# A decoder layer on one core: where the masks, the first splits, the sums and the turns of x stand in the first FFN

## The chip, the core and the metric

The kernel runs on one core of a Trainium2 chip. A core has five engines, each with its own in-order queue: TensorE (PE, matrix products; PEld is its weight load), VectorE (DVE), ScalarE (ACT), GpSimd (POOL) and SyncE (SP, which here issues DMAs). Engines wait for each other through semaphores. The metric is the device time of one execution in microseconds (us); the median of several runs counts.

## The reference

One layer of a decoder trunk in float32: 16 meta tokens and 1024 real ones, width 1024, FFN width 2816. Cut to what matters:

```python
h = h + 0.5 * swiglu(rms_norm(h, ffn1_norm[l]), ffn1_w_in[l], ffn1_w_out[l])
u = rms_norm(h, mix_norm[l]) @ w_in[l]
o_hg = hgrn2(...)              # gated linear recurrence, 4 heads, lower bound lb from two rows of logits
o_sb = stick_breaking(...)     # causal attention, 8 heads
h = h + concat[o_hg, o_sb] @ w_out[l]
h = h + 0.5 * swiglu(rms_norm(h, ffn2_norm[l]), ffn2_w_in[l], ffn2_w_out[l])

def swiglu(h, w_in, w_out):
    g, u = jnp.split(h @ w_in, 2, axis=-1)
    return (jax.nn.silu(g) * u) @ w_out
```

## The kernel before, in words

**Products.** Every float32 operand is split in two: a rounded high part (an ACT copy into the type fp32r) and the rest (a DVE subtraction). A product of two operands takes three matmuls: high by high, low by high, high by low. The FFNs use a fast 2 x 2 block scheme with seven products instead of eight: the activations give the operands B11, B21, B22 and the sums T1 to T4, the weights four blocks and the sums S1 to S4. Weight sums are made by POOL from loaded blocks (`made`, L380, in `fast_in`), split by ACT (L356) and DVE (L358), and used by 12 matmuls of 128x128 by 128x512 (`times`, L426).

**The first FFN's input pass** (`fast_in`, called in `run`). Hidden columns are taken in pairs of *quads*: for each of the gate and the up half a quad makes seven products into the PSUM banks qa, qb, qc. The first four pairs, eight quads q0 to q7, are *opened*: their B11 and B21 products are made while the operands are still being prepared (`open_tokens`). Their later five products follow in `in_turns`, which takes one step of each of the two quads of a pair in each round: first the weight S2, then T2, T3, T1, T4, B22. After each opened pair `between()` is called twice. Seven further pairs run quad by quad, with `between()` after each quad.

**Orders.** TensorE's order in this stage is the one in which the program is written (`manual_schedule`). In `open_tokens` the same holds for ACT, DVE and SP. There a list of items, number 2 to 15, runs between the opened products: item i first prepares a weight for item i+2, then does `items[i]`, then the product of item i. Items 8 to 11 (`combine`) make T3's plain tiles `t3` (L797, L798), items 12 to 15 (`second`) make T2 and split it (`halve`, L306 on ACT, L307 on DVE). After the last item a loop splits the other operands in the order T3, T1, T4, B22; for T4 it first subtracts in place, `sub(b21[j], b21[j], t2[j])` (L853). Elsewhere in the stage the tile framework orders the queues of ACT, DVE, POOL and SP itself, by readiness and by place in the program. `issue_after(x)` puts an instruction behind x on x's engine.

**What starts when the opening is over** (`open_ev` in `run`). `setup_rest` loads the small vectors, makes `ident_b`, `neg_b` and the seven masks of the recurrence (for each level a DVE memset of `sd`, four POOL selects, L119 and L123, and a DVE cast to `masks`, L127), and the few operations on the lower bound's logits. Then the pool of the opening's plain tiles (b11, b21, b22, t2, t3) is closed and new pools take its space: the evictions, `turn_x` (row and result of a transposed piece of x) and `early` (blocks loaded early; the second quad of an opened pair takes its raw blocks and sums from it). A tile in a reused place waits until the old tile's last reader is done.

**Two side jobs run inside the pass.** `turn_x` turns x by TensorE in 18 pieces, one in each `between()`: the first call loads a row (`xrow`, one buffer), each later call transposes it (L918), copies it out (L922), stores it (L923) and loads the next. `split_ahead` splits weights of later stages ahead of time and stores both parts in DRAM; for the second FFN's first columns `quad_group` makes the sums S1 to S4 on POOL (L197), with their split on ACT (L172) and DVE (L173).

**The output pass** (`fast_out`) follows with eleven steps q for each of seven block products, beginning with step "A12". Each q loads a weight block (`raw`) and an activation (`act`), splits both (`halved`, L605 on ACT and L606 on DVE) and makes 12 matmuls (L660). `self.apart` is true in the first FFN and false in the second. The norm before the mixer ends with casts in `norm_steps` (L1755), after which `self.lb` and `self.lbc`, two sigmoids of `self.mx` (L1936, L1937), are written in the program; the recurrence's gates use them later.

Of the kernel before, what the change touches and what calls it, by code (L numbers as in the profile page):

```python
# [15 lines left out]
AF = mybir.ActivationFunctionType  # L16
# [24 lines left out]
class Block:  # L41
# [59 lines left out]
    def setup_rest(self):  # L101

        nc = self.nc
        for dst, src in self.loads:
            nc.sync.dma_start(dst, src)
        nc.vector.tensor_copy(self.ident_b, self.ident)
        nc.vector.memset(self.neg_b, 0.0)
        nc.gpsimd.affine_select(
            out=self.neg_b, in_=self.neg_b, pattern=[[-1, P]],
            compare_op=ALU.is_gt, fill=NEG, base=0, channel_multiplier=1,  # L110
        )
        sd = self.sd
        for i, n in enumerate(LEVELS):
            nc.vector.memset(sd, 1.0)
            nb = P // (2 * n)
            for h in range(2):
                v = sd.rearrange("s (b h r) -> s b h r", h=2, r=n)[:, :, h, :]
                at = n * (1 - h)
                nc.gpsimd.affine_select(  # L119
                    out=v, in_=v, pattern=[[-2 * n, nb], [0, n]],  # L120
                    compare_op=ALU.is_ge, fill=0.0, base=-at, channel_multiplier=1,
                )
                nc.gpsimd.affine_select(  # L123
                    out=v, in_=v, pattern=[[2 * n, nb], [0, n]],
                    compare_op=ALU.is_gt, fill=0.0, base=at + n, channel_multiplier=-1,
                )
            nc.vector.tensor_copy(self.masks[:, i, :], sd)  # L127

        nc.vector.tensor_scalar_mul(self.qg8, self.qg, 1.0 / 8.0)
        l0, l1, mx = self.l0, self.l1, self.mx  # L130
        nc.vector.tensor_max(mx, l0, l1)
        nc.vector.tensor_sub(l0, l0, mx)
        nc.vector.tensor_sub(l1, l1, mx)
        nc.vector.tensor_sub(mx, l0, l1)

    def weights(self, name, raw, split, ctx, on_vector=False):
        self.wp = self.pool(name, ctx=ctx)
# [48 lines left out]
    def quad_group(self, pool, w_in, col, dst):  # L186

        nc = self.nc
        views = [
            w_in[512 * h : 512 * h + 512, col + P * i : col + P * i + P]  # L190
            .rearrange("(k p) f -> p k f", p=P) for i, h in ((0, 0), (1, 0), (1, 1), (0, 1))
        ]
        s = {}

        def kept(name, op, x, y):
            t = s[name] = pool.tile([P, 512], F32, tag="sum", name="sum", bufs=2)
            op(t, x, y)  # L197
            return t

        add, sub = nc.gpsimd.tensor_add, nc.gpsimd.tensor_sub  # L200
        return views, [
            (dst[0], lambda r: r[0]),
            (dst[1], lambda r: r[3]),
            (dst[4], lambda r: kept(1, add, r[1], r[2])),
            (dst[2], lambda r: kept(2, sub, s[1], r[0])),
            (dst[6], lambda r: kept(4, sub, r[3], s[2])),
            (dst[5], lambda r: r[2]),
            (dst[3], lambda r: kept(3, sub, r[0], r[1])),
        ]
# [136 lines left out]
    def fast_in(self, ops, n, w_in, actD, openers, ev0, open_ev, feed=None, meta=None, spare=None,  # L346
                between=lambda: None, after_opened=lambda: None, taken=lambda at, step=True: None):

        nc = self.nc
# [194 lines left out]
            ]  # L544

        def in_turns(live):
            while live:
                live = [q for q in live if next(q, live) is not live]

        opened = [q for f in range(0, 2 * openers, 2) for q in pair(f, "first")]  # L550
        if feed:
# [10 lines left out]
        ev["p"] = open_ev()  # L562
        for i in range(0, 2 * openers, 2):
            in_turns(opened[i : i + 2])
            between()
            between()
        after_opened()
        for f in range(2 * openers, D_FF // P, 2):
# [4 lines left out]
    def fast_out(self, hT, cs, n, w_out, actD, ready, between=lambda a, q: None,  # L573
                 meta=lambda a, q, blocks: None):

        nc = self.nc
# [24 lines left out]
        def halved(src, name, m):  # L601
            i = turns[name]
            turns[name] = (i + 2) % 8
            hi, lo = (self.parts[name][:, j, :m] for j in (i, i + 1))
            nc.scalar.copy(hi, src)  # L605
            nc.vector.tensor_sub(lo, src, hi.bitcast(F32))  # L606
            return hi, lo

        sub = nc.vector.tensor_sub
# [36 lines left out]
        for bank, a, b, start, (i, j) in steps:  # L646
            if start:
                banks[bank] = [
                    pout.tile([P, n], F32, tag=f"{bank}{m}", name="o") for m in range(4)
                ]  # L650
            for q in range(nq):
                src, blocks = left(a, q)
                wh, wl = halved(src, "w", 512)
                xh, xl = halved(right((q, b), n), "t", n)
                order = [(m, e) for m in range(4) for e in range(3)]
                if a == "A12" and q == 0:
                    order.sort(key=lambda me: me[1])
                for m, e in order:
                    y, z = ((wh, xh), (wl, xh), (wh, xl))[e]
                    nc.tensor.matmul(  # L660
                        banks[bank][m], y[:, m * P : (m + 1) * P], z,
                        start=start and q == 0 and e == 0,
                        stop=q == nq - 1 and e == 2, skip_group_check=True,
                    )
# [52 lines left out]
    def open_tokens(self, ops, opened, rows_at, pool, operands):  # L717
# [92 lines left out]
        def second(j):  # L810
            if j == 0:
                rows_at.close()
                operands()
            sub(t2[j], b22[j], b11[j])
            self.halve(ops["T2"], t2[j], j)

        def roots():
            for i, row in enumerate(rb + [meta]):
# [9 lines left out]
        def sums(i):  # L828
# [6 lines left out]
            5: roots,  # L835
            6: lambda: (spare(4, 5), scales()),
            7: keep_b22,
            12: lambda: second(0), 13: lambda: second(1),
            14: lambda: second(2), 15: lambda: second(3),
        }  # L840
        items.update({8 + j: lambda j=j: combine(j) for j in range(4)})
        after = {6: turn_b22, 7: turn_b12, 8: turn_meta}
        for i in range(2, len(order)):
            if i + 2 < len(order):
                next(order[i + 2])
            items[i]()
            next(order[i])
            after.get(i, lambda: None)()
        left = iter((("T3", t3), ("T1", b11), ("T4", b21), ("B22", b22)))
        for o, b in left:  # L850
            for j in range(4):
                if o == "T4":
# [715 lines left out]
    def run(self):  # L1568
# [12 lines left out]
        n = 512  # L1581
# [8 lines left out]
        with ExitStack() as c0:  # L1590
            with ExitStack() as c1:
# [122 lines left out]
                with tc.manual_schedule(engines={nc.tensor.engine}), ExitStack() as c2:  # L1714
# [17 lines left out]
                    def norm_steps(t0, banks, engines, wait, turn):  # L1732

                        acc = pn.tile([P, n], F32, tag="nacc", name="nacc", bufs=2)
                        for k in range(KT):
                            self.square(acc, hT, k, t0, n, pn, engines[k % 2])
                            nc.gpsimd.dma_start(hD[k, :, t0 : t0 + n], hT[:, k, t0 : t0 + n])
                            yield
                        for _ in range(wait):
                            yield  # L1740
                        r = self.inv_rms_rows(acc, n, pn, *banks()[0])
                        for _ in range(turn):
                            yield
                        ps = self.spread_rows(r, n, pn, *banks()[1])
                        rs = pn.tile([P, n], F32, tag="spread", name="rs", bufs=2)
                        nc.scalar.copy(rs, ps)
                        yield
                        for k in range(KT):
                            t = pn.tile([P, n], F32, tag="nt", name="nt", bufs=2)
                            nc.vector.scalar_tensor_tensor(  # L1750
                                t, hT[:, k, t0 : t0 + n], self.gm[:, k : k + 1], rs,
                                ALU.mult, ALU.mult,
                            )
                            xh, xl = hat
                            nc.scalar.copy(xh[:, k, t0 : t0 + n], t)  # L1755
# [180 lines left out]
                nc.scalar.activation(self.lb, self.mx, AF.Sigmoid)  # L1936
                nc.scalar.activation(self.lbc, self.mx, AF.Sigmoid, scale=-1.0)  # L1937

                def after_early():
                    pe_ctx.close()  # L1940
# [233 lines left out]
```

## Time and profile before

| | us |
|---|---|
| median of 3 runs (2066.33 to 2069.84) | 2068.24 |
| profiled execution | 2067.01 |
| its span, from first to last instruction | 2065.3 |
| first FFN, input pass: first product to first product of the output pass | 15.9 to 532.7 |
| TensorE busy in the span | 1982.5 |

The profile gives start and length of each instruction on each engine, and for idle time what ended it (the releaser). "Granted clock" is the share of TensorE's full clock that it was given. A row of a stretch gives its length and then the busy time of PE, PEld, DVE, ACT and POOL, with instruction counts in brackets, then the granted clock, the share of the DMA engines and GB/s. A row of waits reads: who waited, for whom, total us, times, longest. A row of the order of time reads: start, length, engine, line, operation, what it writes and reads, count, and in square brackets the idle time ahead of it with its releaser.

### The profile page before, as it was taken

To read this page: it belongs to the slowest core of one execution; us is meant where nothing else is said; L and a number is where in the kernel's file an instruction comes from. 1 tells how busy PE (TensorE), PEld (TensorE's weight loads), DVE (VectorE), ACT (ScalarE), POOL (GpSimd) and SP (SyncE) were. 2 spreads that over 40 slices of the span, in tenths; PEclk is the share of its full clock that TensorE was granted. 3 is DMA by queue.
4 is the path that set the end of the run, shared out by engine and by line. 5 is a ranking of instruction groups with operands and counts; after the bars stand their busy time and mean duration, and the time that the engine had idled before them with its cause. 6 is when DMAs were issued, how large, how long until landed. Compare 5 with 4: busy or idle time off the path is not lost.

```text
span 2065.3 us, 30888 instructions
## 1 busy us (share of the span) xinstructions
PE 1982.5 (96%) x11004; PEld 1659.6 (80%) x11004; DVE 1361.4 (66%) x1988; ACT 867.7 (42%) x1758; POOL 672.8 (33%) x768
## 2 busy tenths in 40 slices
PE   7598999999999999999999998999999999999998
PEld 6387788777788888888889887878888888888887
DVE  6675467887677764235767668548576776676774
ACT  6332334333344443446666654535033233234443
POOL 0466345665200001224333323321264464440000
PEclk9799999999999999999999999999999999999999
DMA  6144487764896522634454337684633332359463
GB/s 185 56 129 147 148 263 247 260 227 164 276 328 228 166 94 87 206 125 137 121 140 132 100 109 246 167 242 156 203 118 95 112 105 94 107 217 321 131 199 137
DMA packets 283097, 347.18 MB, mean 168 GB/s; under 512 B 28016, under 2 KB 183152, under 8 KB 282944
## 3 DMA queue, kind: packets, MB, share of 16 engines
q1 hardware_dynamic: 263376, 287.98, 44.1%
q0 software_dynamic: 18528, 57.23, 7.9%
q8 instruction: 87, 1.43, 0.3%
q14 instruction: 66, 0.54, 0.1%
q10 hardware_dynamic: 1040, 0.00, 0.0%
HBM read 233.75 MB, written 111.38 MB: 167 GB/s over the span
## 4 chain that ended last, share of the span: by engine, by line
PE 68%; DVE 4%; DMA 2%; ACT 1%; issue 1%; SPq 0%; DVEq 0%
PE o L660 18%; PE qb L426 9%; PE qc L426 6%; PE qa L426 6%; PE proj L247 5%; PE proj L249 5%; PE proj L248 5%; PE flip L1300 2%; PE wo L248 1%; PE wo L247 1%; PE wo L249 1%; DMA raw<-in_ffn_w_out_dram 1%; PE lvl L1096 1%; PE oacc L1370 1%; PE oacc L1372 1%
## 5 line engine op out<-in xcount | busy, mean ns | idle before, releaser
L426 PE MATMUL qb<-T,wh 128*128 128x512 f32 x1056 | 350.4, 396 | 31.5 <-ACT wh L356 24.7
L426 PEld LDWEIGHTS qb<-T,wh 128*128 128x128 f32 x1056 | 201.7, 191 | 80.2 <-ACT wh L356 27.2
L358 DVE TENSOR_TENSOR wl<-s,wh 128x512 fp32r<-128x512 f32 x160 | 209.5, 1310 | 80.9 <-ACT wh L356 79.4
L426 PE MATMUL qa<-B,wh 128*128 128x512 f32 x696 | 229.7, 394 | 0.6 <-ACT B L755 0.2
L660 PE MATMUL o<-t,w 128*128 128x512 f32 x924 | 215.9, 394 | 2.8 <-DVE t L606 1.8
L247 PE MATMUL proj<-xh,wh 128*128 128x512 f32 (+2 forms) x640 | 216.6, 338 | 0.8 <-DVE st L996 0.7
L249 PE MATMUL proj<-xl,wh 128*128 128x512 f32 (+2 forms) x640 | 209.7, 328 | 0.8 <-DVE xl L1756 0.8
L660 PE MATMUL o<-parts 128*128 128x512 f32 x924 | 210.2, 389 | 0.1
L248 PE MATMUL proj<-xh,wl 128*128 128x512 f32 (+2 forms) x640 | 210.0, 328 | 0.0
L426 PE MATMUL qb<-T,wl 128*128 128x512 f32 x528 | 208.7, 395 | 0.3 <-DVE wl L358 0.3
L660 PEld LDWEIGHTS o<-t,w 128*128 128x128 f32 x924 | 173.4, 189 | 42.3 <-DVE t L606 3.1
L356 ACT CAST wh<-s 128x512 fp32r<-128x512 f32 x160 | 99.5, 622 | 253.3 <-PE qb L426 152.6
L660 PEld LDWEIGHTS o<-parts 128*128 128x128 f32 x924 | 173.3, 188 | 36.4 <-DVE parts L606 0.5
L380 POOL TENSOR_TENSOR s<-raw 128x512 f32<-128x512 f32 x80 | 110.9, 1387 | 140.1 <-DMA raw<-in_ffn_w_in_dram 90.5
L426 PEld LDWEIGHTS qa<-B,wh 128*128 128x128 f32 x696 | 131.3, 189 | 29.5 <-ACT both L450 0.9
L426 PE MATMUL qa<-B,wl 128*128 128x512 f32 x348 | 136.0, 391 | 0.0
L249 PEld LDWEIGHTS proj<-xl,wh 128*128 128x128 f32 x640 | 120.5, 188 | 12.2 <-DVE xl L1756 1.2
L247 PEld LDWEIGHTS proj<-xh,wh 128*128 128x128 f32 x640 | 120.8, 189 | 11.4 <-DVE st L996 1.2
L248 PEld LDWEIGHTS proj<-xh,wl 128*128 128x128 f32 x640 | 120.7, 189 | 9.1
L358 DVE TENSOR_TENSOR wl<-raw,wh 128x512 fp32r<-128x512 f32 x120 | 117.5, 980 | 13.7 <-ACT wh L356 13.5
L356 ACT CAST wh<-raw 128x512 fp32r<-128x512 f32 x120 | 74.4, 621 | 123.5 <-PE qc L426 86.4
L1452 POOL TENSOR_TENSOR sig<-sig,keep 128x144 f32<-128x144 f32 (+3 forms) x64 | 81.4, 1272 | 133.6 <-DVE keep L1446 82.4
(387 smaller groups left out, 4118.6 us busy)
## 6 DMA issues: line engine op xcount, KB each, us to landing
raw<-in_ffn_w_in_dram SPq DMA_DIRECT2D x176, 256.0 KB, 3.8
raw<-in_ffn_w_out_dram SPq DMA_DIRECT2D x121, 256.0 KB, 4.3
w2in<-both SPq DMA_DIRECT2D x28, 512.0 KB, 3.2
raw<-in_w_in_dram SPq DMA_DIRECT2D x25, 512.0 KB, 4.0
ks<-kD SPq DMA_DIRECT2D x32, 260.0 KB, 4.9
wout<-both SPq DMA_DIRECT2D x16, 512.0 KB, 4.1
wh<-w2in SPq DMA_DIRECT2D x27, 256.0 KB, 3.4
wl<-w2in SPq DMA_DIRECT2D x27, 256.0 KB, 3.4
```

The costliest lines, as they stand in the source:

```text
L247: nc.tensor.matmul(ps, wh[:, s], xs, start=k == 0, stop=False)
L248: nc.tensor.matmul(ps, wl[:, s], xs, start=False, stop=False)
L249: nc.tensor.matmul(ps, wh[:, s], xl[:, k, c0 : c0 + n], start=False, stop=k == nk - 1)
L356: nc.scalar.copy(hi, src)
L358: nc.vector.tensor_sub(lo, src, hi.bitcast(F32))
L380: taken(op(t, x, y), False)
L426: nc.tensor.matmul(ps, a[:, k, :], b[:, k, :], start=start and k == 0 and i == 0, stop=k == 3 and i == 2, skip_group_check=True,)
L660: nc.tensor.matmul(banks[bank][m], y[:, m * P : (m + 1) * P], z, start=start and q == 0 and e == 0, stop=q == nq - 1 and e == 2, skip_grou ...
L1096: nc.tensor.matmul(ps[:, :, c, :], kp[:, P * c : P * c + P], strided(QA, P * c + n, (512 - n, 2), (2 * n, nb), (1, n)), start=True, stop=True,
L1300: self.nc.tensor.transpose(ps[:m, j, :], src[:, s0 : s0 + m], self.ident)
L1370: nc.tensor.matmul(o[:, c], vj, w[0], start=j == 0, stop=False, skip_group_check=True)
L1452: nc.gpsimd.tensor_mul(sig, sig, keep[:, 1 : nk + 1])
```

## The change

The masks leave `setup_rest` and become a generator `setup_masks`, taken one step at a time in items 5 to 15 of `open_tokens`, after `items[i]()` and ahead of the item's product. T3 is split in `second(j)`, right behind T2, and leaves the loop at the end. In `in_turns` the third round of a pair (after T3's products) is followed by one `between()`, and one of the two after the pair is dropped. `quad_group` makes its sums on DVE. In the first FFN's output pass the splits of steps q = 0 to 2 of "A12" get high priority, and the activation's load is written ahead of the weight's split. The two sigmoids are put behind the last cast of the norm.

```diff
         for dst, src in self.loads:
             nc.sync.dma_start(dst, src)
+        nc.vector.tensor_scalar_mul(self.qg8, self.qg, 1.0 / 8.0)
+        l0, l1, mx = self.l0, self.l1, self.mx
+        nc.vector.tensor_max(mx, l0, l1)
+        nc.vector.tensor_sub(l0, l0, mx)
+        nc.vector.tensor_sub(l1, l1, mx)
+        nc.vector.tensor_sub(mx, l0, l1)
+
+    def setup_masks(self):
+        nc = self.nc
         nc.vector.tensor_copy(self.ident_b, self.ident)
         nc.vector.memset(self.neg_b, 0.0)
         nc.gpsimd.affine_select(
             out=self.neg_b, in_=self.neg_b, pattern=[[-1, P]],
             compare_op=ALU.is_gt, fill=NEG, base=0, channel_multiplier=1,
         )
+        yield
         sd = self.sd
         for i, n in enumerate(LEVELS):
             nc.vector.memset(sd, 1.0)
...
+            yield
             nc.vector.tensor_copy(self.masks[:, i, :], sd)
-
-        nc.vector.tensor_scalar_mul(self.qg8, self.qg, 1.0 / 8.0)
...
-        add, sub = nc.gpsimd.tensor_add, nc.gpsimd.tensor_sub
+        add, sub = nc.vector.tensor_add, nc.vector.tensor_sub
...
         def in_turns(live):
+            rounds = 0
             while live:
                 live = [q for q in live if next(q, live) is not live]
+                rounds += 1
+                if rounds == 3:
+                    between()
...
         for i in range(0, 2 * openers, 2):
             in_turns(opened[i : i + 2])
-            between()
             between()
...
-                wh, wl = halved(src, "w", 512)
-                xh, xl = halved(right((q, b), n), "t", n)
+                act = right((q, b), n)
+                with self.tc.high_priority() if self.apart and a == "A12" and q < 3 else ExitStack():
+                    wh, wl = halved(src, "w", 512)
+                    xh, xl = halved(act, "t", n)
...
             sub(t2[j], b22[j], b11[j])
             self.halve(ops["T2"], t2[j], j)
+            self.halve(ops["T3"], t3[j], j)
...
+        masks = self.setup_masks()
         after = {6: turn_b22, 7: turn_b12, 8: turn_meta}
         for i in range(2, len(order)):
             if i + 2 < len(order):
                 next(order[i + 2])
             items[i]()
+            if i > 4:
+                next(masks, None)
             next(order[i])
             after.get(i, lambda: None)()
-        left = iter((("T3", t3), ("T1", b11), ("T4", b21), ("B22", b22)))
+        left = iter((("T1", b11), ("T4", b21), ("B22", b22)))
...
-                            nc.scalar.copy(xh[:, k, t0 : t0 + n], t)
+                            self.last_cast = nc.scalar.copy(xh[:, k, t0 : t0 + n], t)
...
-                nc.scalar.activation(self.lb, self.mx, AF.Sigmoid)
-                nc.scalar.activation(self.lbc, self.mx, AF.Sigmoid, scale=-1.0)
+                with tc.issue_after(self.last_cast.ins):
+                    nc.scalar.activation(self.lb, self.mx, AF.Sigmoid)
+                    nc.scalar.activation(self.lbc, self.mx, AF.Sigmoid, scale=-1.0)
```

More of the change, by code (lines that the diff above doesn't have):

```diff
@@ L126, in setup_rest @@
                 )
+            yield
             nc.vector.tensor_copy(self.masks[:, i, :], sd)
-        nc.vector.tensor_scalar_mul(self.qg8, self.qg, 1.0 / 8.0)
[L130 to L134, printed above, removed]
     def weights(self, name, raw, split, ctx, on_vector=False):
@@ L837, in open_tokens @@
             7: keep_b22,
-            12: lambda: second(0), 13: lambda: second(1),
-            14: lambda: second(2), 15: lambda: second(3),
         }
+        items.update({12 + j: lambda j=j: second(j) for j in range(4)})
         items.update({8 + j: lambda j=j: combine(j) for j in range(4)})
+        masks = self.setup_masks()
         after = {6: turn_b22, 7: turn_b12, 8: turn_meta}
```

## The prediction

> **What bounds the kernel now.** I read the page first, then the busy time by stretches of 20 us, then the waits of TensorE, and last the order of time at each gap.
>
> ```profile
> span 2065.3 us, 30888 instructions
> PE 1982.5 (96%) x11004; PEld 1659.6 (80%) x11004; DVE 1361.4 (66%) x1988; ACT 867.7 (42%) x1758; POOL 672.8 (33%) x768
> ```
>
> ```profile
> 60.00:80.00 20.00, 9.21 (x38) 6.62 (x37) 15.59 (x34) 12.03 (x23) 5.69 (x10) 0.82 0.19 62
> 80.00:100.00 20.00, 5.58 (x12) 4.13 (x13) 11.24 (x22) 4.45 (x8) 13.93 (x25) 0.50 0.19 55
> 140.00:160.00 20.00, 17.18 (x105) 14.20 (x104) 13.07 (x15) 6.81 (x13) 14.56 (x12) 0.95 0.41 131
> 160.00:180.00 20.00, 20.00 (x142) 16.34 (x142) 9.22 (x12) 4.72 (x11) 9.55 (x10) 0.96 0.48 157
> 180.00:200.00 20.00, 16.55 (x71) 13.42 (x70) 12.32 (x14) 5.73 (x10) 16.20 (x16) 0.91 0.38 127
> 220.00:240.00 20.00, 17.32 (x75) 14.16 (x74) 8.08 (x11) 5.30 (x9) 10.53 (x12) 0.91 0.40 143
> ```
>
> ```profile
> PE qb L426 <- ACT wh L356: 24.7, 1, 24.7
> PE xt L918 <- DMA xrow<-in_x_dram: 8.9, 3, 3.5
> PE qb L426 <- DVE actm L875: 4.0, 3, 1.8
> ```
>
> TensorE works in 96% of the span, so only its gaps and its slow clock can be won. The stretches (columns: length, PE, PEld, DVE, ACT, POOL, granted clock, DMA) show one long gap between 60 and 100 us and three short ones between 140 and 240; the waits name them: 24.7 us in one piece, 8.9 us in three. All lie in the first FFN, which the change rewrites.
>
> **The change part by part.** The sum is made against the profiled execution, 2067.01 us, which is 1.2 below the median of the runs shown.
>
> *A. Masks and T3 splits moved among the opened products.* The long gap, engine by engine:
>
> ```profile
> 68.25 2.48 DVE L307 TENSOR_TENSOR T<-t,T 128x512 fp32r<-128x512 f32 x4
> 75.03 0.73 DVE L853 TENSOR_TENSOR b<-b,t 128x512 f32<-128x512 f32 x1
> ```
>
> ```profile
> SPq L369 <- DVE b L853: 21.2, 1, 21.2
> ```
>
> ```profile
> 75.83 2.02 SPq L369 DMA_DIRECT2D raw<-in_ffn_w_in_dram  x4
> ```
>
> ```profile
> DMA to landing us min/median/max: 2.9/3.4/4.6
> ```
>
> ```profile
> L119 POOL TENSOR_SCALAR_AFFINE_SELECT sd<-sd 128x64 f32<-128x64 f32 x14 | 6.6, 492 | 4.8 <-DVE sd L114 4.1 <-DVE mx L134 0.7
> L123 POOL TENSOR_SCALAR_AFFINE_SELECT sd<-sd 128x64 f32<-128x64 f32 x14 | 5.5, 412 | 0.0
> ```
>
> ```profile
> 90.78 1.26 POOL L380 TENSOR_TENSOR s<-raw 128x512 f32<-128x512 f32 x1
> 92.12 1.26 POOL L380 TENSOR_TENSOR s<-s,raw 128x512 f32<-128x512 f32 x1
> ```
>
> ```profile
> 94.08 0.79 PE L426 MATMUL qb<-T,wh 128*128 128x512 f32 x1 [24.73 <-ACT wh L356]
> ```
>
> TensorE has done one T2 product and stands from 69.35 to 94.08 for the weight of the second. That weight is a sum of three blocks, which POOL makes only at 90.78, behind 28 selects for the masks (12.1 us of work that alternates with DVE). The masks are not the only lock, though. SP issued the four block loads at 75.83, after 21.2 us behind a subtraction of L853, the one that ends at 75.03 + 0.73: their buffers take the place of the opening's tiles. With the selects gone, **these loads are what is late next**, and I time that chain. Room on DVE and ACT ahead of it:
>
> ```profile
> 40.00:57.00 17.00, 17.00 (x89) 14.14 (x88) 10.62 (x16) 6.09 (x11) 3.01 (x3) 1.00 0.32 94
> 57.00:68.00 11.00, 10.85 (x47) 8.34 (x46) 8.54 (x12) 5.99 (x12) 2.36 (x3) 1.00 0.06 24
> ```
>
> ```profile
> L127 DVE CAST masks<-sd 128x128 uint8<-128x128 f32 x7 | 2.6, 375 | 6.2 <-POOL sd L123 6.2
> ```
>
> ```profile
> 54.48 1.30 POOL L380 TENSOR_TENSOR s<-raw 128x512 f32<-128x512 f32 x1 [11.33 <-DMA raw<-in_ffn_w_in_dram]
> ```
>
> The masks bring DVE 7 casts (2.6 us) and 7 memsets (taken as no dearer), two steps each from item 5 to item 13 of the written order; most fall before 57 us, where DVE has 6.4 us free and POOL works 3.0 of 17. I cost that part at nothing. Without that room its price would be these 5.2 us in front of the weight splits. From 57 us on DVE is tight: 2.5 us free, and those are round trips to ACT within each T2 split. Here land the four T3 splits (2.48 us on DVE, about as much on ACT, which has 5.0 free) and the last two masks (about 0.5). A T3 split stands behind its T2 split and so doesn't fill that round trip: the last T2 split slides by about 2 us, to 69.7. That stalls TensorE by 1 to 2 us, but only in front of the longer wait. T3 leaves the queue behind (2.48 us) as it comes in ahead (2.9): L853's second subtraction ends at about 76.2, as now. Loads from 76.3; the third block, which the sum needs, is issued 1.0 later and lands 3.4 to 4.6 after that, at 80.7 to 81.9; then the two sums, the cast and the weight load as now (94.08 - 90.78 = 3.3): TensorE goes on at 84.0 to 85.2. I take 84.5, so **-9.5** of the 24.7. The slow clock behind it stays:
>
> ```profile
> 94.00:100.00 6.00, 5.58 (x12) 4.13 (x13) 3.37 (x3) 1.17 (x3) 3.94 (x3) 0.50 0.01 1
> ```
>
> Bounds: -27.6 if a buffer were free early (24.7, and 2.9 for the half clock in these 5.6 us); -4 or worse if DVE falls behind, since its mask casts now wait on POOL in an order that is fixed by hand, with weight splits and T2 halves queued behind them, and POOL's own block sums wait on a DMA until 54.48.
>
> *B. One `between` of each pair moved to the middle of the pair.* Each pair ended in two turns of x, and the second one's row is loaded only after the first one's transposes:
>
> ```profile
> 155.58 4.25 SPq L681 DMA_DIRECT2D xrow<-in_x_dram  x2
> ```
>
> ```profile
> 509.52 2.72 PE qc L426 x12
> ```
>
> Half a pair on there are three rounds of two products, 6 x 2.72 = 16 us, for that load. This cover hides the 8.9 us of waits; gone, they are back. The turns stay the same in number, with their stores and copies. The stretches add a slow clock behind each wait: (0.05 + 0.04 + 0.09 + 0.09) x 20 = 5.4 us of TensorE's time, part of which lies in the waits. **-13.5**, bounds -8.9 and -14.3. [...]
>
> *C. First splits of the output pass first.* The seam between the passes:
>
> ```profile
> 527.27 0.69 DVE L512 TENSOR_TENSOR u<-qc,u 128x512 f32<-128x512 f32 x1 [2.71 <-PE qc L426]
> 535.22 1.78 DVE L606 TENSOR_TENSOR w<-raw,w 128x512 fp32r<-128x512 f32 x1
> 537.52 3.30 DVE L606 TENSOR_TENSOR w<-raw,w 128x512 fp32r<-128x512 f32 x1
> ```
>
> ```profile
> 528.45 0.62 ACT L605 CAST t<-act 128x512 fp32r<-128x512 f32 x1
> ```
>
> ```profile
> 532.65 4.14 PE L660 MATMUL o<-t,w 128*128 128x512 f32 x13
> 543.17 4.15 PE L660 MATMUL o<-t,w 128*128 128x512 f32 x10 [1.79 <-DVE t L606]
> 547.25 0.86 PE L1768 MATMUL m<-raw,actm 128*32 128x128 f32 x24
> ```
>
> The first 36 products (three steps) take 532.65 to 547.25, 14.6 us, where 36 x 2.72 / 12 = 8.2 would do: 6.4 lost. ACT has its casts done by 529.1, but DVE's halves stand behind the last evictions, although DVE idles before them (2.71 us once), and then stretch to 3.30. Six halves of about 0.65 fit into these idle times. The fourth step's still lie behind. **-4.5**, bounds -6.4 and +2 (a split at the head of a queue that waits for its own load, with the last weights' casts behind it).
>
> *D. Sums for later weights by DVE.*
>
> ```profile
> L197 POOL TENSOR_TENSOR sum<-early x8: 1287/1443/1743, 357.7 to 505.3; 128x512 f32<-128x512 f32 x8
> ```
>
> ```profile
> L173 DVE TENSOR_TENSOR both<-sum,both x16: 676/686/5436, 381.1 to 516.7; 128x512 fp32r<-128x512 f32 x16
> ```
>
> ```profile
> 350.00:520.00 170.00, 164.49 (x916) 132.94 (x915) 136.55 (x143) 64.56 (x123) 109.00 (x97) 0.99 0.62 214
> ```
>
> Sixteen sums leave POOL (about 23 us) and add 16 x 0.69 = 11 us to DVE, which has 33.5 of 170 free. TensorE loses 5.5 there, some of it behind DVE instructions stretched to 5.4 us while POOL works. [...] I take **-2**, bounds -5.5 and +4.
>
> *E. The gates' sigmoids moved behind the last cast.* A table load and two short activations leave a place off the path and come to one where TensorE already waits for ACT:
>
> ```profile
> L1936 ACT ACT_TABLE_LOAD x1 | 1.3, 1283 | 0.0
> ```
>
> ```profile
> 796.72 0.66 PE L1300 MATMUL flip<-ident,vTs 128*128 128x128 f32 x4 [1.33 <-ACT vTs L1210]
> ```
>
> **+1**, bounds 0 and +2.
>
> Sum: -9.5 - 13.5 - 4.5 - 2 + 1 = -28.5; 2067.0 - 28.5 = 2038.5, and 1.2 for the median: **2040**.
>
> **The rivals.** *The loads aren't late* (0.10): the wait behind L853 goes with the masks, A is -27.6, the time 2022. For it: T3's tiles come free earlier. Against: L853 keeps its place in DVE's order. *The opening pays* (0.13): POOL's block sums, which wait for a DMA until 54.48 and end near 59, stand ahead of mask levels; DVE stops up to 11 us at a mask cast, 6.4 of which it had free, so A shrinks to between -5 and +2: 2044 to 2051. For it: both share one in-order queue. Against: most levels are asked for before 54. *The turns still wait* (0.09): SP holds the row's load behind block loads that wait for buffers; B is 0, the time 2053. For it: SP's 21.2 us on one wait; against: 16 us of room. *Slower: DVE becomes the bound* (0.08): each moved sum is stretched as the worst split beside it, 5.4 us; 16 x 5.4 = 87 against 33.5 free, 53 over, less the other 26.5: 2094. It decides from (33.5 + 26.5) / 16 = 3.75 us per sum; the median of 686 ns speaks against it.
>
> **How the numbers follow.** My forecast has 0.60, alone 2030 to 2050. The range 2022 to 2056 takes in the first three rivals. Faster by over 0.2% (what a measurement here can tell from no change) 0.90, the same 0.02 from the edges, slower 0.08.
>
> **What would show it.** A: no mask select between 70 and 90 us, block loads still issued near 76, and a TensorE wait of 13 to 16 us that ends with them. If that wait is under 5, the first rival holds; over 20, the second. B: no wait on `xrow`, clock 1.00 from 140 to 240. C: first 36 products of the output pass in under 11 us. D: sums of 0.7 to 1.4 us on DVE, TensorE busy for over 165 of the same 170 us. E: a table load near 760. A longer gap at 30 to 66 us, or DVE near full from 320 to 490, would prove me wrong.

## The result, and the profile after

The changed kernel takes 2053.72 us (median of 4 runs, 2053.23 to 2054.86) against 2068.34 beside it; the ratio is 0.9931, with a 95% interval of 0.9914 to 0.9948. 2040 was predicted: the sign and the range hold, and about half of the expected gain came, 14.6 of 28.5 us. The time lies outside the 2030 to 2050 that the forecast alone would have given. The profiled executions differ by 12.15 us (2067.01 and 2054.86).

The page of the changed kernel, first lines:

```profile
span 2053.2 us, 30869 instructions
PE 1980.8 (96%) x11004; PEld 1659.7 (81%) x11004; DVE 1365.5 (67%) x2004; ACT 867.2 (42%) x1758; POOL 656.9 (32%) x752
```

Its waits of TensorE (in all, times, longest):

```profile
PE qb L430 <- ACT wh L360: 14.9, 1, 14.9
...
PE qb L430 <- DVE u L462: 6.6, 2, 3.8
PE wo L251 <- DMA wh<-wout: 2.9, 2, 1.9
...
PE qb L430 <- DVE wl L362: 2.5, 1, 2.5
PE o L669 <- DVE w L613: 2.3, 3, 1.2
...
PE o L669 <- ACT w L612: 1.6, 1, 1.6
```

And its busy time by stretches of 20 us:

```profile
140.00:160.00 20.00, 20.00 (x91) 16.53 (x90) 17.42 (x19) 6.33 (x11) 16.12 (x16) 1.00 0.25 89
...
220.00:240.00 20.00, 20.00 (x120) 16.54 (x119) 13.08 (x17) 9.50 (x18) 9.42 (x10) 1.00 0.53 165
...
420.00:440.00 20.00, 16.17 (x76) 12.44 (x78) 16.26 (x16) 5.11 (x10) 14.44 (x15) 0.91 0.45 173
532.00:552.00 20.00, 18.18 (x112) 13.94 (x111) 8.09 (x13) 7.48 (x14) 1.20 (x2) 0.91 0.91 316
```

The long wait is 14.9 in place of 24.7 us, and the one on `xrow` is gone, with a granted clock of 1.00 in all five stretches from 140 to 240 us. But waits stand here that the list of before has not or has smaller: on `u` (1.3 before), on `wl`, on `wh<-wout`, and on the output pass's `w`. The 4.0 us on `actm` of before are gone.

A total doesn't say where time was won and where it was given back. TensorE's order of products is the same in both kernels where they are compared here, so one product's start can be set against its own start in the other trace:

| one and the same product | before, us | after, us | difference | since the row above |
|---|---|---|---|---|
| first one with T2 (opening) | 66.47 | 68.26 | +1.8 | |
| first on the meta tokens (behind the opening's gap) | 105.61 | 100.09 | -5.5 | -7.3 |
| ninth on the meta tokens (four opened pairs done) | 242.93 | 224.39 | -18.5 | -13.0 |
| eighteenth | 434.25 | 412.67 | -21.6 | -3.0 |
| first of the output pass | 532.65 | 515.40 | -17.3 | +4.3 |
| first on the meta tokens there (three steps done) | 547.25 | 525.80 | -21.5 | -4.2 |
| last `m` (output pass and norms done) | 775.47 | 760.91 | -14.6 | +6.9 |
| last `nps` (end of the mixer) | 1420.07 | 1408.01 | -12.1 | +2.5 |
| last of all | 2055.82 | 2043.70 | -12.1 | 0.0 |

The first row's +1.8 us has the size of the stall that the prediction put in front of the long wait (1 to 2 us), though TensorE waits there twice for a copy on ACT (0.84 and 0.58 us) and not for the last T2 split. Of the -3.0 down to the eighteenth, 1.7 us are three short waits of before on `u` and `actm`; the rest wasn't followed. Three places give time back: 4.3 us between 412 and 515, 6.9 in the output pass, 2.5 in the mixer. The first is seen on three engines (changed kernel, order of time: start, length, engine, and at the end what ended the idle time before it):

```profile
430.84 3.46 DVE L362 TENSOR_TENSOR wl<-s,wh 128x512 fp32r<-128x512 f32 x1
434.22 0.68 DVE L462 TENSOR_TENSOR u<-qb,p 128x512 f32<-128x512 f32 x1
...
431.25 1.28 POOL L533 TENSOR_TENSOR t<-sg,t 128x512 f32<-128x512 f32 x1
432.47 1.27 POOL L540 TENSOR_TENSOR sg<-sg 128x512 f32<-128x512 f32 x1
...
435.04 0.47 PE L430 MATMUL qb<-T,wh 128*128 128x512 f32 x1 [3.83 <-DVE u L462]
```

A weight split that takes 0.68 us at 437.79 takes 3.46 here, while POOL makes two subtractions back to back. Behind it on DVE stands `u`, which empties the PSUM bank that TensorE's next product needs: 3.83 us of wait, and a granted clock of 0.91 in that stretch. The same pattern comes again at 481 us. (The 4.3 us are a net figure: before the change two waits on `actm`, 1.84 and 1.68 us, stood in this stretch.)

The second is on SP's queue and in what follows from it:

```profile
525.80 0.86 PE L1780 MATMUL m<-raw,actm 128*32 128x128 f32 x24
...
526.89 0.47 SPq L622 DMA_DIRECT2D ak<-in_ffn_w_out_dram  x1
528.46 0.32 SPq L603 DMA_DIRECT2D act<-act110B  x1
529.03 0.32 SPq L1869 DMA_DIRECT2D hT<-xD  x1
529.72 2.25 SPq L598 DMA_DIRECT2D raw<-in_ffn_w_out_dram  x3
...
537.46 0.51 PE L669 MATMUL o<-t,w 128*128 128x512 f32 x1 [1.60 <-ACT w L612]
```

The products on the meta tokens (`m`, at 525.80) free the buffers of the pass's first three weight blocks. The blocks of steps 6 to 8, which want them, are issued only at 529.72: in front of them on the queue stand loads for the pass's next stages (`ak`, `hT`) and an activation (`act110B`), ahead of which the queue issues nothing from 527.36 to 528.46. TensorE reaches step 6 and waits, 1.60 us.

### The profile page after: what moved, and what is told of

Same layout as the page of the kernel before. It is cut to its first block, busy times and chain, and to the rows that moved or that the text cites. A ratio compares the mean times of both kernels' runs of the same rounds, so it can differ in the third digit from the quotient of the medians.

```text
span 2053.2 us, 30869 instructions
## 1 busy us (share of the span) xinstructions
PE 1980.8 (96%) x11004; PEld 1659.7 (81%) x11004; DVE 1365.5 (67%) x2004; ACT 867.2 (42%) x1758; POOL 656.9 (32%) x752
## 4 chain that ended last, share of the span: by engine, by line
PE 67%; DVE 3%; DMA 2%; ACT 1%; issue 1%; SPq 0%; DVEq 0%; ACTq 0%
PE o L669 18%; PE qb L430 9%; PE qc L430 6%; PE qa L430 6%; PE proj L251 5%; PE proj L253 5%; PE proj L252 5%; PE flip L1312 2%; PE wo L251 1%; PE wo L252 1%; PE wo L253 1%; DMA raw<-in_ffn_w_out_dram 1%; PE lvl L1108 1%; PE oacc L1382 1%; PE oacc L1384 1%; PE z L1448 1%
## 5 line engine op out<-in xcount | busy, mean ns | idle before, releaser
L430 PE MATMUL qb<-T,wh 128*128 128x512 f32 x1056 | 349.6, 395 | 22.8 <-ACT wh L360 14.9
L430 PEld LDWEIGHTS qb<-T,wl 128*128 128x128 f32 x528 | 100.6, 191 | 23.8 <-DVE wl L362 3.4
```

The costliest lines, as they stand in the source:

```text
L430: nc.tensor.matmul(ps, a[:, k, :], b[:, k, :], start=start and k == 0 and i == 0, stop=k == 3 and i == 2, skip_group_check=True,)
```

## Experiments: each part undone

Four variants of the changed kernel ran beside the kernel before, each with one part taken back. Ratios are to the kernel before; 0.9931 (0.9914 to 0.9948) is the change itself. Where an interval overlaps this one, the times alone don't tell the two kernels apart, and what is said of them rests on the traces.

**Masks back in one piece behind the opening** (T3's splits stay where the change put them):

```diff
             nc.sync.dma_start(dst, src)
+        drain(self.setup_masks())
...
-        masks = self.setup_masks()
...
-            if i > 4:
-                next(masks, None)
```

> The changed kernel with the masks made where they stood before, once the opening is over (the T3 splits stay among the opened products). Theory: in the changed kernel the masks' new place is worth about 5.5 us at the first gap (TensorE reaches the meta products after it 5.52 us earlier), so 2059, and the gap again ends near 95 us with POOL's block sums behind the selects. Rival: the T3 splits alone bring it, since they let the block loads go; then about 2054 and a gap that ends near 90.

Measured: 2059.35 us, ratio 0.9957 (0.9943 to 0.9972).

```profile
94.48 0.80 PE L431 MATMUL qb<-T,wh 128*128 128x512 f32 x1 [23.66 <-ACT wh L361]
95.60 0.79 PE L431 MATMUL qb<-T,wl 128*128 128x512 f32 x1 [0.33 <-DVE wl L363]
```

The old gap is back, and the kernel is 5.4 us (0.0026 of 2068) slower than the change, so the T3 splits alone don't bring the gain. They do bring the later start of T2: its first product stands at 67.94 here, 1.5 us later than before. The second row matters as well: TensorE waits 0.33 us for the weight's low half (`wl`) here, and 2.45 in the changed kernel. So of the 8.5 us by which the moved masks bring the first product forward (94.48 to 86.03), 2.1 are lost again at once.

**Both turns of x at the end of a pair**:

```diff
-                if rounds == 3:
+                if rounds == 0:
                     between()
...
             between()
+            between()
```

> The changed kernel with both turns of x at the end of each opened pair, as before. Theory: the three waits on the row's load and the slow clock behind them come back, 13 to 14 us, so 2067. Rival: the row's load was late only because of what SP had in front of it at that time; then under 5 us, 2058.

Measured: 2066.47 us, ratio 0.9994 (0.9982 to 1.0007).

```profile
PE xt L931 <- DMA xrow<-in_x_dram: 9.3, 3, 3.9
```

This part alone is worth 0.0063 of 2068, 13.0 us, and in the traces the stretch from the first to the ninth product on the meta tokens is 13.1 us longer: 9.3 of waits, and the slow clock behind them (0.91 in each of the stretches 140 to 160, 180 to 200 and 220 to 240).

**Sums for later weights on GpSimd again**:

```diff
-        add, sub = nc.vector.tensor_add, nc.vector.tensor_sub
+        add, sub = nc.gpsimd.tensor_add, nc.gpsimd.tensor_sub
```

> The changed kernel with the sums for later weights on POOL again. Theory (as predicted): the move is worth 2 to 3 us, so 2056, with small TensorE gaps spread over 355 to 490 us. Rival: DVE pays for them, and the two TensorE gaps at 431 and 480 us in the changed kernel (together some 8 us) are theirs; then 2049 to 2051 and none of these gaps.

Measured: 2055.62 us, ratio 0.9933 (0.9913 to 0.9953). The time is the one that the theory names, but beside its own runs of the kernel before it is 0.4 us (0.0002 of 2068) behind the change, and both traces span 2053.2 us: the move can't be told from nothing. The waits on `u` at 435 and 481 us are gone, and one of its own stands in their place, behind a split that takes 7.92 us while POOL has five sums and subtractions in a row:

```profile
478.90 7.92 DVE L362 TENSOR_TENSOR wl<-raw,wh 128x512 fp32r<-128x512 f32 x1
...
487.57 0.67 PE L430 MATMUL qb<-T,wh 128*128 128x512 f32 x1 [3.91 <-DVE actm L887]
```

So the sums' place decides where the wait falls, not whether there is one: from the ninth product on the meta tokens to the output pass's first it is 290.7 us here, 291.0 in the changed kernel and 289.7 before.

**No priority for the first splits of the output pass**:

```diff
-                with self.tc.high_priority() if self.apart and a == "A12" and q < 3 else ExitStack():
+                with self.tc.high_priority() if False else ExitStack():
```

> The changed kernel with the output pass's first splits in their old place in the queues. Theory: the seam loses its 4.2 us (first 36 products 14 to 15 us instead of 10.4), but the weight block of step 6 is no longer late behind the loads for the next step, so that the 6.9 us that the output pass lost after the seam are not lost: 2051. Rival: that later loss has nothing to do with the splits' place; then the seam alone shows, 2058.

Measured: 2051.44 us, ratio 0.9919 (0.9896 to 0.9942): no slower than the change. In the trace the seam takes 13.2 us in place of 10.4 (first `m` at 528.37, not 525.80), and from there to the last `m` it is 4.0 us faster: 231.15 us, where the changed kernel takes 235.11 and the one before 228.22. So the priority wins 2.8 of the seam's 4.2 us, and the same pass gives back 4.0. The theory's time came, but from smaller parts than it named: 2.8 lost for 4.2, and 4.0 won for 6.9.

## Experiments: the opening's chain

**The four in-place subtractions of T4's operand first, then all splits.** They release the opening's buffers for the block loads, and in the changed kernel each waits for the split in front of it.

```diff
+        for j in range(4):
+            sub(b21[j], b21[j], t2[j])
         for o, b in left:
             for j in range(4):
-                if o == "T4":
-                    sub(b21[j], b21[j], t2[j])
                 self.halve(ops[o], b[j], j)
```

> The changed kernel with the four in-place subtractions of the T4 operand (0.68 us each, at 73.94, 75.92, 77.89 and 79.87 us in the changed kernel, each a cast apart) done together ahead of T1's splits. Theory (TensorE's wait of 14.89 us is set by the block loads, and they by the last of these subtractions): the loads issue some 4 us earlier, TensorE resumes near 83 in place of 86 and its second wait is met by DVE's remaining splits, 3 us are gained, about 2050.5 against 2053.7. Rival (what ends the stall is DVE's queue of splits up to the low half, whose work is not changed): the first wait gets shorter and the second longer by the same, under 1 us gained, 2053 to 2054.

**B22's splits out of that list**, to be placed freely:

```diff
-        left = iter((("T1", b11), ("T4", b21), ("B22", b22)))
+        left = iter((("T1", b11), ("T4", b21)))
...
+        self.b22_splits = lambda: [self.halve(ops["B22"], b22[j], j) for j in range(4)]
...
```

> The changed kernel with the splits of B22 taken out of the list behind the opened products; they are planned freely and land among the opened products' splits, ahead of T2's. Theory (TensorE's second wait of 2.45 us and the half clock behind it come from the low half's place behind B22's splits, which take 5.70 us while GpSimd makes the block sums): the second wait goes, the first stays within 1 us, 2 to 4 us are gained, 2050 to 2052. Rival (GpSimd's sums stretch whatever DVE does at that time, the low half included, or the earlier splits delay the opened products as much): the second wait moves only, 2053 to 2054.

**Both**:

> Both of the edits above in one kernel. Theory (two links of one chain: subtractions, loads, sums, casts, then the low half): the gains add up to 5 to 7 us, TensorE resumes near 82 with no second wait, 2047 to 2049. Rival (one bound behind both): the same time as the better of the two alone.

| | time, us | ratio | first product on the meta tokens against the changed kernel |
|---|---|---|---|
| subtractions first | 2051.48 | 0.992 (0.9906 to 0.9933) | -4.7 us |
| B22's splits early | 2052.09 | 0.9927 (0.9914 to 0.9941) | -2.0 us |
| both | 2048.71 | 0.9907 (0.9893 to 0.992) | -4.9 us |

Each of these intervals overlaps that of the change itself (0.9914 to 0.9948), so the gains are read from the traces. The changed kernel first, in order of time:

```profile
76.67 2.02 SPq L373 DMA_DIRECT2D raw<-in_ffn_w_in_dram  x4
...
81.84 5.70 DVE L311 TENSOR_TENSOR B<-b,B 128x512 fp32r<-128x512 f32 x4
...
81.95 1.71 POOL L384 TENSOR_TENSOR s<-raw 128x512 f32<-128x512 f32 x1 [9.47 <-DMA raw<-in_ffn_w_in_dram]
83.73 1.59 POOL L384 TENSOR_TENSOR s<-s,raw 128x512 f32<-128x512 f32 x1
...
86.03 0.80 PE L430 MATMUL qb<-T,wh 128*128 128x512 f32 x1 [14.89 <-ACT wh L360]
89.28 0.80 PE L430 MATMUL qb<-T,wl 128*128 128x512 f32 x1 [2.45 <-DVE wl L362]
```

With the subtractions first:

```profile
73.10 2.09 SPq L373 DMA_DIRECT2D raw<-in_ffn_w_in_dram  x4
...
78.97 2.49 DVE L311 TENSOR_TENSOR B<-b,B 128x512 fp32r<-128x512 f32 x4
...
78.37 4.21 POOL L384 TENSOR_TENSOR s<-raw 128x512 f32<-128x512 f32 x1 [5.69 <-DMA raw<-in_ffn_w_in_dram]
...
84.62 0.79 PE L430 MATMUL qb<-T,wh 128*128 128x512 f32 x1 [13.26 <-ACT wh L360]
85.83 0.79 PE L430 MATMUL qb<-T,wl 128*128 128x512 f32 x1 [0.41 <-DVE wl L362]
```

The loads are issued 3.57 us earlier, as the theory has it, yet TensorE goes on only 1.41 us earlier: now POOL's first sum takes 4.21 us, and B22's four splits on DVE beside it their usual 2.49. In the changed kernel it is the other way round: those splits take 5.70 us, and the sum 1.71. In both kernels one of the two engines takes much longer while the other works beside it, and which one differs. Of the 4.7 us these are 1.4; the second wait, 2.45 to 0.41, is 2.0; and the rest is the half clock, which ends sooner (granted clock 0.85 in place of 0.66 from 84 to 100 us).

With B22's splits early alone, that second wait goes as well:

```profile
83.22 1.26 POOL L384 TENSOR_TENSOR s<-raw 128x512 f32<-128x512 f32 x1 [9.74 <-DMA raw<-in_ffn_w_in_dram]
...
86.53 0.80 PE L430 MATMUL qb<-T,wh 128*128 128x512 f32 x1 [14.38 <-ACT wh L360]
87.65 0.80 PE L430 MATMUL qb<-T,wl 128*128 128x512 f32 x1 [0.33 <-DVE wl L362]
```

So B22's splits, standing beside POOL's sums and ahead of the low half, caused it. With no split beside it the first sum takes 1.26 us again. But the early splits have a price ahead of the gap, here with both edits:

```profile
60.33 0.47 PE L430 MATMUL qa<-B,wh 128*128 128x512 f32 x1 [2.38 <-DVE sum L513]
```

In the changed kernel the same product follows without a wait. Both edits together bring hardly more at the opening than the subtractions alone, 4.9 for 4.7 us, as the rival's number has it, but not for its reason: TensorE goes on at 83.48, 1.1 us sooner than with the subtractions alone, and the opened products in front of the gap end 1.1 us later. (The times differ by more, 2.8 us; their intervals overlap, and what is behind the opening wasn't followed.)

## Experiments: the output pass's loads

**Activations, A11's blocks and rows of the hidden state behind the weight block of the ninth step**, by order of issue only (`behind()` is `issue_after` that block's load; one of its places is shown):

```diff
-                nc.sync.dma_start(a, block(0, 0, q))
+                with behind():
+                    nc.sync.dma_start(a, block(0, 0, q))
...
```

> The changed kernel with the loads of the output pass's next step (weight blocks of A11, activations from the ninth step on, rows of the hidden state) put on SP's queue behind the weight block of A12's ninth step. Theory (the 4 us won at the seam are lost because those loads stand ahead of the weight blocks of steps 6 to 8, which are issued at 529.72, 3 us after their buffers are free): they issue near 526.7, TensorE's wait of 1.60 us at 537.46 and the half clock of that stretch (0.91) go, the seam's gain stays, 3 to 4 us less, about 2050. Rival (the DMA share of 0.91 in that stretch is the bound, the order only moves the wait to the next step): 2053 to 2054.

Measured: 2053.17 us, ratio 0.9931 (0.9918 to 0.9943), no gain.

```profile
537.00 0.32 SPq L222 DMA_DIRECT2D wh<-win  x1
537.42 2.27 SPq L598 DMA_DIRECT2D raw<-in_ffn_w_out_dram  x3
```

```profile
PE o L678 <- ACT w L620: 5.5, 1, 5.5
```

The place that came free on the queue was filled by weights of the next stage, which wait for buffers of their own until 537.00, and the three blocks came 7.7 us later still. TensorE waited 5.5 us in one piece, yet the pass took only 0.7 us more than in the changed kernel (235.83): the changed kernel's four waits there, 3.9 us in all, are gone. That is no test of the rival; the next run is.

**The next stage's weights held back too**:

```diff
     def col_tile(self, w, col):
+        with self.tc.issue_after(self.raw8.ins) if self.raw8 else ExitStack():
...
```

> The changed kernel with everything that SP's queue issued ahead of the weight blocks of the output pass's steps 6 to 8 (blocks of A11, activations from the ninth step on, rows of the hidden state, and the loads of the next stage's weights, which took the free place in the first try of this) put behind the block of the ninth step. Theory (the seam's gain is lost to the place of those loads): the three blocks issue within 1 us of the products on the meta tokens that free their buffers, TensorE's waits on w between 535 and 600 us (1.60, 0.22, 0.87, 1.22 us and the half clock of one stretch) go, from the first product on the meta tokens to the last one of the pass 3 to 5 us less than the 235.1 us of the changed kernel, about 2050. Rival (the pass is bound by the bytes: DMA share 0.91 and more for 80 us): the waits move to later steps, under 1 us gained.

Measured: 2049.74 us, ratio 0.9902 (0.9888 to 0.9916).

```profile
524.30 0.86 PE L1793 MATMUL m<-raw,actm 128*32 128x128 f32 x24
...
524.79 1.28 SPq L602 DMA_DIRECT2D raw<-in_ffn_w_out_dram  x3
...
752.53 0.29 PE L1849 MATMUL m<-ms,ones_d 128*128 128x16 f32 x2
```

```profile
532.00:552.00 20.00, 20.00 (x141) 15.47 (x141) 11.18 (x18) 8.06 (x15) 0.00 (x0) 1.00 1.02 377
```

The blocks are issued 0.5 us after the products that free their buffers. From the first `m` to the last it is 228.23 us, as before the change (228.22) and 6.9 less than with it. The seam's gain stays. With a DMA share of 1.02 TensorE is busy without a break in that stretch, so bytes don't bound the pass; the order in which they are asked for does.

## Experiments: the waits in the middle

**All four subtractions of the combined products on DVE**, so that POOL doesn't work beside the split:

```diff
-                sub = nc.gpsimd.tensor_sub
+                sub = (nc.gpsimd if feed else nc.vector).tensor_sub
```

> The changed kernel with the four subtractions behind each pair of tiles of the first half (up's combined products T1 to T4) on DVE in place of GpSimd, in this FFN alone. Theory (the waits of 3.83 us at 435 and 2.75 us at 481 come from DVE's split of 128x512 that takes 3.46 us in place of 0.68 while GpSimd makes those subtractions back to back; the bank's eviction stands behind it): no DVE split over 2 us near there, both waits go with their half clock, 4 to 5 us gained, about 2049. Rival (DVE has too much to do once it makes the sums, whoever makes the rest; 2.7 us more a pair): the waits on u stay or grow, others come, 2054 to 2060.

Measured: 2072.68 us, ratio 1.0023 (1.0013 to 1.0032), slower than before.

```profile
PE qb L430 <- DVE u L462: 16.6, 7, 5.2
```

```profile
266.36 0.69 DVE L533 TENSOR_TENSOR t<-sg,t 128x512 f32<-128x512 f32 x1 [3.49 <-DMA act14T<-t]
266.96 0.68 DVE L462 TENSOR_TENSOR u<-qb,p 128x512 f32<-128x512 f32 x1
...
267.80 0.77 PE L430 MATMUL qb<-T,wh 128*128 128x512 f32 x1 [3.75 <-DVE u L462]
```

The rival named the sign but not the cause. DVE isn't short of time: it is idle for 3.49 us here, and in the same way for 5.01 and 4.62 at the next two such places. The fourth subtraction writes a buffer that a store still reads, and on DVE it stands in front of `u`. At the two places of the theory the waits don't go, but shrink from 3.83 to 1.93 and from 2.75 to 0.70 us; with the slow clock behind them (0.66 from 435 to 440 us and 0.69 from 481 to 486 in the changed kernel), TensorE is done with the next block product 3.0 and 3.5 us sooner.

**The same with the opening's and the output pass's edits**:

> Both of the edits of this call and the subtractions of the opening done first, in one kernel. If all three theories hold, their gains add up: 4.7 us at the opening, 4 to 5 in the middle, 3 to 5 in the output pass, 2040 to 2043. If DVE becomes the bound with the products' subtractions, 2046 to 2052; if the bytes bound the output pass, 2044 to 2047.

Measured: 2060.04 us, ratio 0.9957 (0.9945 to 0.997): above all three sums, with waits on `u` of 16.1 us in 7 pieces, the mishap of the run above.

**Three of the subtractions on DVE, the fourth on GpSimd, with the other two edits**:

```diff
+                sub = nc.gpsimd.tensor_sub
                 put("T4", made(sg[1, 0], t2))
```

> The changed kernel with the opening's subtractions done first, with the loads held behind the weight block of the output pass's ninth step, and with the first three of the combined subtractions on DVE; the fourth, which waits for a store to free its buffer, stays on GpSimd. Theory (the failure of the run with all four on DVE came from that fourth one, which stood at the head of DVE's queue until the store was done, and the waits at 435 and 481 us come from DVE and GpSimd working at the same time): no wait on u over 1 us between 100 and 500 us, the middle gains 4 us, with 4.7 at the opening and 6.9 in the output pass 15 us less than the changed kernel, about 2038. Rival (DVE has too much to do with the sums and the subtractions): the middle loses, TensorE's waits on u add up to 8 us or more, 2045 to 2055. If the subtractions change nothing in the middle: 2042.

Measured: 2039.31 us (2036.29 to 2041.76), ratio 0.9862 (0.9844 to 0.988), the fastest kernel here.

```profile
PE qb L434 <- DVE u L466: 3.1, 5, 1.9
```

```profile
429.14 0.69 DVE L544 TENSOR_TENSOR sg<-sg 128x512 f32<-128x512 f32 x1
429.74 0.68 DVE L366 TENSOR_TENSOR wl<-s,wh 128x512 fp32r<-128x512 f32 x1
430.34 0.68 DVE L466 TENSOR_TENSOR u<-qb,p 128x512 f32<-128x512 f32 x1
```

The split that took 3.46 us takes 0.68, though the subtractions now stand in front of it (the third of them in the first row), and `u` follows at once. Against the changed kernel the same products come 4.9 us earlier behind the opening, 8.9 at the output pass's first, 15.1 at its last `m`: 4.9, 4.0 and 6.2 where 4.7, 4 and 6.9 were expected. One wait on `u` stays over the 1 us of the expectation (1.9), and the first opened pairs lose 1.8 us again (-4.92 to -3.15). The two runs with all four on DVE lose the same 1.8 there, the run with the opening's edit alone loses none, so it is a price of the moved subtractions.

## Why the prediction was right, and where its sum was off

The direction was right and so were the largest two mechanisms, A and B. That the time fell into the range is partly luck: 2053.7 lies 2 us inside an edge that was drawn to take in rivals, and the rival that stands at 2053, "the turns still wait", isn't what happened, for no wait on `xrow` is left. In the traces 12.1 us came in place of 28.5. The missing 16.4 are about 4.0 in A, 0.5 in B, 7.2 in C, 3.3 in the stretch of D and 2.5 in the mixer, which the sum left out; E gave 1 back.

*A, right in mechanism, too large: -5.5 for -9.5.* The masks went, and the loads behind L853 were what is late next: issued at 76.67 (predicted 76.3), summed from 81.95 (80.7 to 81.9), with a wait of 14.9 us (13 to 16). The step that failed is "then the two sums, the cast and the weight load as now (94.08 - 90.78 = 3.3)". That price is from a place where DVE had its splits behind it. Now sums and splits fall together: the way from sum to product took 86.03 - 81.95 = 4.1 us, and the low half, which the step leaves out, came another 2.45 late. Of the 4.0 us these are 0.8 and 2.1 (0.33 us of that second wait stood there before); the rest is loads and sums that came at the late end of what was expected, and a longer half clock (granted 0.50 for 9.0 us from the product on, 2.4 of them the second wait; before the change for 5.9, 0.3 of them a wait). With B22's splits early, the second wait went and the way took 86.53 - 83.22 = 3.3 us again.

*B, right: -13.0 for -13.5.* The run with the turns put back lost 13.0 us. The term held because it took the clock behind each wait into the sum; the waits alone are 8.9. In the trace of before, behind the waits of 2.82, 3.45 and 2.68 us, the granted clock is 0.86 (160 to 165 us), 0.66 (195 to 200) and 0.69 (230 to 235). Waits of 2.75 and 2.62 us in the run with the turns put back stand in stretches with a clock of 0.91, and so does in the changed kernel a wait of 1.60 us (at 537.46, with one of 0.22 behind it; 0.79 from 540 to 545).

*C, right where it looked: -4.2 for -4.5; wrong over the pass, +6.9.* The first 36 products took 10.4 us, under 11; without the priority 1.4 of the seam's 4.2 us came all the same, for a reason that stays open. The step that failed is "The fourth step's still lie behind": it followed the splits no further and didn't ask what the faster start does to SP's queue. Steps 6 to 8 met their blocks late. With only the order of the loads changed, all 6.9 us came back, so this was the prediction's largest single error. That the priority itself made the planner choose the worse order isn't shown; without it the pass still took 2.9 us more than before the change (the activation's load stayed ahead of the weight's split in that run).

*D, -2 predicted, none that can be measured.* The sums took twice the 0.69 us taken for them (1337 ns each for the eight in the row below), and TensorE was busy for 163.4 of 170 us where over 165 was the mark, and 164.5 before:

```profile
L201 DVE TENSOR_TENSOR sum<-early 128x512 f32<-128x512 f32 x8 | 10.7, 1337 | 0.0
```

```profile
331.00:501.00 170.00, 163.42 (x912) 133.37 (x911) 135.29 (x158) 65.13 (x123) 88.83 (x81) 0.98 0.62 216
```

The step that failed is the one from less work on POOL to less wait of TensorE. The stretch doesn't go with POOL's sums; it goes with the four subtractions, which stayed where they were, and with what stands behind the stretched split. Taking three of them off POOL won 4.0 us there, where D was to win 2. That 2 was the author's estimate, and no run shows it: with the sums back on GpSimd the span is 2053.2 us, as with them on DVE. Why an instruction takes longer beside one of the other engine isn't shown either; which one pays, 5.70 us on DVE or 4.21 on POOL, only the traces told.

*E, +1 predicted, 0.* The product behind the early projections stands 14.6 us ahead on either side of it. The table load came at 773.46, not near 760, and delayed nothing.

*Left out:* 2.5 us in the mixer, where TensorE waits for output weights (`wh<-wout`, 2.9 us in the changed kernel, none in the one before, 0.9 to 2.6 in the variants), with a granted clock of 0.91 from 1260 to 1280. The same stretch took 644.6 us before, 647.1 with the change and 644.0 to 647.0 in the variants, so no part of the change is shown to cause it. That loads meet other work there when all is earlier is only a guess; it wasn't tried.

Of the rivals, "the opening pays" came nearest in size for A (-5 at best), but not in cause: the last selects end at 65.2 us, none lies between 70 and 90, and the wait that came was DVE's own.

## What to carry to other kernels

Whoever makes a stage start earlier should list what each queue then holds in front of that stage's next loads: here the change won 4 us at a seam and lost 6.9 in the same pass until the loads were put in order. A duration from a row is only worth something with the neighbour's state beside it; a split of 0.68 us on DVE took 3.46 here while GpSimd made two subtractions back to back. And before an instruction is moved to a busier queue, ask what it waits for: one subtraction of four, which waits for a store, turned a gain of some 4 us into a loss.

## What was not expected of the hardware

In these runs DVE and GpSimd took longer beside each other, in both directions, on fp32 instructions with two inputs of 128x512: a DVE split took 3.46 us in place of 0.68 with GpSimd at its usual 1.27 to 1.28 (and 7.92 in the run with the sums on GpSimd again), and a GpSimd sum took 4.21 in place of 1.26 with DVE's four splits at their usual 2.49. In the first case the split ended at 434.30 us, GpSimd's two subtractions at 433.74; in the second the sum ended at 82.58, DVE's four splits at 81.46 and a small maximum behind them at 82.60.
